# Attention scores in pairs of PSUM banks, the head norm's multiply on GpSimd, and low-order weights over all 128 rows

## Chip, cores and metric

The kernel runs on one core of a Trainium2 chip. The metric is the device time of one execution in microseconds; lower is better.

## What is computed

One inference step of one encoder layer, on 1024 prompt rows and 64 sample rows of width 1024. The normalised input goes through one input projection; its columns feed two groups of heads, whose gated outputs go through one output projection:

```
A) differential attention, 8 heads (q1, q2, k1, k2 of 64, value of 128), chunks of 64 seen block-causally:
   s   = q_c . k_c / 8            c = 0, 1      masked by chunk
   p_c = softmax(s)                             over up to 1024 keys (sample: 64 + 128 cached)
   o   = (p_0 - lam * p_1) @ v
   o   = rms_norm(o) * subln * (1 - lambda_init) * silu(gate)
B) RWKV-7 mixing, 16 heads of 64:
   decay = f(w0 + tanh(wd) @ w_up)      a = sigmoid(a0 + ad @ a_up)      (wd, ad of rank 64)
   a matrix state per head is updated row by row with decay, a, k, v; its output is normed and gated
```

## The kernel before

One stream of instructions per engine is written out ahead of time by a planner, the class `Weave`: generators (streams with a rank) yield a delay or a condition, the planner runs the ready stream of lowest rank, and `spend` and `op_` tell it what a piece costs TensorE or another engine. So the order on each engine's queue is fixed when the kernel is built, and the planned costs decide it. On the chip each queue runs in order.

Phase B comes first. `unit` (n = 0 to 16) handles one pair of B heads and one half of 512 prompt rows, 16 units in all, and one unit for the sample rows. A unit computes decay and rate, inverts its chunk matrices, and then walks a chain of 8 chunks, in which TensorE (`cbank`, L804, L821, L832) and VectorE (`gsb` L818, `suv` L827, L828, L842) answer each other. Units overlap. The `filler` stream has the lowest rank: it puts the input projections of both groups (`proj_cm`, L215 to L217, 384 or 320 columns a matmul) between the steps of the units.

The decay and rate inputs are matrix products in two parts. `xw` holds the high part of tanh(wd) in rows 0 to 63 and its low part in rows 64 to 127; `xa` holds the rate input with the halves the other way about. The weights `t` hold w_up and a_up twice, once in each half of the rows: slices 0 and 1 are the rounded weights, slices 2 and 3 what the rounding left. Line 513 multiplies the rounded weights over all 128 rows, line 514 the remainders over the 64 rows `r` of the input's high part.

Phase A follows. For each of 8 heads, `prep` loads q, k, v and the gate and splits q and k into two parts each (`qs`, `k1`, `k2`, L1244 to L1252; map 0 on VectorE, map 1 on GpSimd). Each head has 9 tiles of queries: `qt` 0 to 7 sees 128 to 1024 keys, and `qt` 8 is the sample with 192. `score` runs once for each tile and map c: keys in pieces of up to 512, each piece in one PSUM bank of a pool of four (`pss`), two matmuls a piece (L1322, L1323), a masking memset (L1330), a maximum per piece (L1332), for two pieces the minimum of the two negated maxima (L1337), and an exponential per piece (L1348) that also sums its row. `at["free"]` counts banks for the planner. `qtile` then joins the two maps: for two pieces it adds their sums (L1364), takes reciprocals, combines the maps (`e`, L1370), transposes the weights in blocks of 128 (L1381) into `wt` (L1385), multiplies with the values (L1395), scales (L1403), squares and sums (L1407), makes the norm on GpSimd (`ms`, L1409, L1410), and multiplies by it on VectorE (L1412). After 4 tiles `on` is transposed (L1419) and gated (L1424).

`out_projection` fills the gaps of phase A and the time after it: weights and mixed rows are loaded and split (`wor`, `mxr`, L157 and L158), and multiplied (L1145 to L1147, 512 columns a matmul).

Of the kernel before, what the change touches and what calls it, by code (L numbers as in the profile page):

```python
# [11 lines left out]
F32 = mybir.dt.float32  # L12
# [46 lines left out]
class Weave:  # L59
# [13 lines left out]
    def spend(self, ns):  # L73
        self.now += ns
# [207 lines left out]
def phase_b(tc, I, O, E):  # L282
# [8 lines left out]
    with ExitStack() as bs:  # L291
# [184 lines left out]
        def unit(n, p, hf):  # L476
# [21 lines left out]
            for q0 in range(0, 8, 4) if smp else (0,):  # L498
                if smp:
                    ups = [load_up(q) for q in range(q0, q0 + 4)]  # L500
                    yield W_DMA
                for i, raw in enumerate(ups):
                    ups[i] = t = t512(dt=F32R, nm=f"wus{u}{q0 + i}").rearrange("p (s c) -> p s c", c=P)
                    nc.scalar.copy(t[:, 0:2], raw[:, 0:2])
                    op_(ACT, 256)
                    gtt(t[:, 2:4], raw[:, 0:2], t[:, 0:2].bitcast(F32), op=SUB)
                    d = op_(POOL, 256)
                yield d
                for q, t in enumerate(ups):
                    for j, (x, r) in enumerate(((xw, slice(0, 64)), (xa, slice(64, 128)))):  # L510
                        o_ = pss2[j][:, (q0 + q) * CH:(q0 + q + 1) * CH] if smp else pss2[j]
                        cl = slice(TP, T) if smp else slice(hf * HALF, (hf + 1) * HALF)
                        mm(o_, t[:, j], x[:, cl], start=True, stop=False)
                        mm(o_, t[r, 2 + j], x[r, cl], start=False, stop=True)
                spend(900)

            sq = t512(nm=f"sq{u}")
# [646 lines left out]
def phase_a(tc, I, O, E):  # L1164
# [7 lines left out]
    QW = 9 * P  # L1172

    ap_ = E["ctx"].enter_context(tc.tile_pool(name="ap", bufs=1, reuse_waits="tile"))
    pss = E["ctx"].enter_context(tc.tile_pool(name="pss", bufs=4, space=PSUM, reuse_waits="tile"))
    psx = E["ctx"].enter_context(tc.tile_pool(name="psx", bufs=2, space=PSUM, reuse_waits="tile"))


# [30 lines left out]

    H = {}  # L1210
    ready = set()
    at = {"s": 0, "free": 4}

    def prep(h):
        yield lambda: h in projected and {("q", h // 4), ("k", h // 4)} <= roped and (h == 0 or (h - 1, 1) in ready) and at["s"] >= 18 * (h - 1) + 10
# [87 lines left out]
    ons = {}  # L1303
    turned, summed = set(), set()

    def score(i, h, qt, c, st):

        k0, n = (0, (qt + 1) * P) if qt < 8 else (TP, TS + PAST)
        u = f"{h}_{qt}{c}"
        j = 2 * i + c  # L1310
        parts = [(o_, min(512, n - o_)) for o_ in range(0, n, 512)]
        m = len(parts)
        yield lambda: at["s"] == j and at["free"] >= m and (h, c) in ready
        at["free"] -= m
        at["s"] = j + 1
        qs, k1, k2 = H[h][0:3]
        ss = []
        lq = qs[c][:, qt * P:(qt + 1) * P]
        for o_, w in parts:
            s = pss.tile([P, 512], F32, tag="s", name=f"s{u}{o_}")  # L1320
            ss.append(s)
            mm(s[:, 0:w], lq, k1[c][:, k0 + o_:k0 + o_ + w], start=True, stop=False)  # L1322
            mm(s[:, 0:w], lq, k2[c][:, k0 + o_:k0 + o_ + w], start=False, stop=True)  # L1323
            spend(w / 1.2 + 20)
        yield LA
        nb = ap_.tile([P, 3], F32, tag=f"nb{c}", bufs=3, name=f"nb{u}")
        for i_, (s, (o_, w)) in enumerate(zip(ss, parts)):
            if qt < 8 and i_ == m - 1:

                nc.vector.memset(s[0:64, w - 64:w], -(2.0 ** 100))  # L1330
                op_(DVE, 60)
            nc.vector.tensor_reduce(nb[:, i_:i_ + 1], s[:, 0:w], axis=AX.X, op=MAX, negate=True)  # L1332
            d = op_(DVE, w)
        mx = nb[:, m - 1:m]
        if m > 1:
            mx = nb[:, 2:3]
            vtt(mx, nb[:, 0:1], nb[:, 1:2], op=ALU.min)  # L1337
            d = op_(DVE, 60)
        yield d
        yield lambda: i < 2 or i - 2 in turned  # L1340
        if "sm" not in st:
            st["sm"] = ap_.tile([P, 2], F32, tag="sm", bufs=3, name=f"sm{u}")
            if m > 1:
                st["sp"] = ap_.tile([P, 2, 2], F32, tag="sp", bufs=3, name=f"sp{u}")
        e = ap_.tile([P, 1024], F32, tag=f"e{c}", bufs=2, name=f"e{u}")
        for i_, (s, (o_, w)) in enumerate(zip(ss, parts)):
            sm = st["sm"][:, c:c + 1] if m == 1 else st["sp"][:, c, i_:i_ + 1]
            act(e[:, o_:o_ + w], s[:, 0:w], AF.Exp, bias=mx, accum_out=sm)  # L1348
            d = op_(ACT, w + 50)
            weave.later(d, free_s)  # L1350
        yield d
        st[c] = e

    def free_s():
        at["free"] += 1
# [1 line left out]
    def qtile(i, h, qt, st):  # L1357
        n = (qt + 1) * P if qt < 8 else TS + PAST
        kbs = [(b * P, P, b) for b in range(qt + 1)] if qt < 8 else [(0, TS, 8), (TS, PAST, 9)]
        u = f"{h}_{qt}"  # L1360
        yield lambda: 0 in st and 1 in st
        w_, e1, sm = st[0], st[1], st["sm"]
        if "sp" in st:
            nc.vector.tensor_reduce(sm, st["sp"], axis=AX.X, op=ADD)  # L1364
            op_(DVE, 60)
        ri = ap_.tile([P, 2], F32, tag="ri", bufs=3, name=f"ri{u}")
        nc.vector.reciprocal(ri, sm)
        co = ap_.tile([P, 1], F32, tag="co", bufs=3, name=f"co{u}")
        vts(co, sm[:, 0:1], nlam, ri[:, 1:2], op0=MUL, op1=MUL)
        stt(w_[:, 0:n], e1[:, 0:n], co, w_[:, 0:n], op0=MUL, op1=ADD)  # L1370
        op_(DVE, 400)
        yield op_(DVE, n)
        yield lambda: (h, 2) in ready
        vn, ga = H[h][3:]
        yield lambda: i < 2 or i - 2 in summed
        wt = ap_.tile([P, 8, P], F32, tag="wt", bufs=2, name=f"wt{u}")
        for b0 in range(0, len(kbs), 4):
            sub = kbs[b0:b0 + 4]
            ps = yield from xps(f"wt{u}{b0}")
            for b, (o_, w, _) in enumerate(sub):  # L1380
                nc.tensor.transpose(ps[0:w, b * P:(b + 1) * P], w_[:, o_:o_ + w], ident)  # L1381
            spend(112 * len(sub))
            yield LA
            if qt < 8:
                (nc.vector.tensor_copy if b0 == 0 else nc.scalar.copy)(  # L1385
                    wt[:, b0:b0 + len(sub), :], ps[:, 0:len(sub) * P].rearrange("p (k q) -> p k q", q=P))
            else:
                for b, (o_, w, _) in enumerate(sub):
                    nc.vector.tensor_copy(wt[0:w, b, :], ps[0:w, b * P:(b + 1) * P])
            d = xdone(op_(DVE if b0 == 0 else ACT, P * len(sub)))  # L1390
        turned.add(i)
        yield d
        ops = yield from xps(f"o{u}")
        for b, (o_, w, vb) in enumerate(kbs):
            mm(ops[:, 0:P], wt[0:w, b, :], vn[0:w, vb, :], start=(b == 0), stop=(b == len(kbs) - 1))  # L1395
        spend(230 * len(kbs))
        summed.add(i)
        yield LA
        j = qt // 4
        if (h, j) not in ons:  # L1400
            ons[h, j] = ap_.tile([P, 4, P], F32, tag="on", bufs=3, name=f"on{u}")
        on = ons[h, j][:, qt % 4, :]
        act(on, ops[:, 0:P], AF.Copy, scale=ri[:, 0:1])  # L1403
        yield xdone(op_(ACT, P))
        sq = ap_.tile([P, P], F32, tag="osq", name=f"osq{u}")
        ms = ap_.tile([P, 1], F32, tag="ms", bufs=3, name=f"ms{u}")
        act(sq, on, AF.Square, accum_out=ms)  # L1407
        yield op_(ACT, P)
        gts(ms, ms, 1.0 / P, SUBLN_EPS, op0=MUL, op1=ADD)  # L1409
        gtt(ms, ms, nh[:, 0:1], op=POW)  # L1410
        yield op_(POOL, 270)
        vts(on, on, ms, None, op0=MUL)  # L1412
        d = op_(DVE, P)
        if qt in ((3, 7, 8) if h < 7 else (0, 4, 8)):
            yield d
            m = 4 if qt < 8 else 1
            ps = yield from xps(f"z{u}")
            for b in range(m):
                nc.tensor.transpose(ps[:, b * P:(b + 1) * P], ons[h, j][:, b, :], ident)  # L1419
            spend(112 * m)  # L1420
            yield LA
            n_ = HALF if qt < 8 else TS
            y = ap_.tile([P, HALF], F32, tag="y", name=f"y{u}")
            stt(y[:, 0:n_], ps[:, 0:n_], hsl, ga[:, j * HALF:j * HALF + n_], op0=MUL, op1=MUL)  # L1424
            xdone(op_(DVE, n_))
            nc.sync.dma_start(out=mixd["A", j][h * P:(h + 1) * P, :], in_=y[:, 0:n_])
            yield 3000
            mixed.add((f"A{h}", j))

    for h in range(8):  # L1430
        weave.add(10 * h + 9.5, prep(h))
        for o_, qt in enumerate((0, 1, 8, 2, 3, 4, 5, 6, 7) if h < 7 else (7, 6, 5, 4, 3, 2, 1, 0, 8)):
            st = {}
            weave.add(10 * h + o_, qtile(9 * h + o_, h, qt, st))
            for c in range(2):
                weave.add(10 * h + o_ + 0.1 * c + 0.1, score(9 * h + o_, h, qt, c, st))
    weave.run(lambda: not weave.live)


# [57 lines left out]
```

## Time and profile before

| what | value |
|---|---|
| median of 3 runs | 1876.28 us (1874.08 to 1876.33) |
| the profiled execution | 1870.95 us, span 1869.1 us |
| mean granted TensorE clock | 0.975 |
| busy: TensorE, weight loads, VectorE, ScalarE, GpSimd | 91%, 80%, 70%, 46%, 37% |
| phase B, attention, the rest of the output projection | about 0 to 1240, 1260 to 1740, 1740 to 1869 us |

A matmul's record begins when its columns enter the array; records of neighbours overlap, since matmuls are pipelined. So the distance from start to start is what a matmul costs the engine, not the length of its record. PE stands for TensorE, PEld for its weight loads, DVE for VectorE, ACT for ScalarE and POOL for GpSimd.

### The profile page before, as it was taken

The numbers are of one execution on the slowest core, as the hardware profiler recorded it, in microseconds if no ns is written. First come the engines' busy times: TensorE is split into PE (matmuls) and PEld (weight loads), VectorE is DVE, ScalarE is ACT, GpSimd is POOL, SyncE is SP. The second block draws the span as 40 slices with busy tenths as digits, with TensorE's granted clock in tenths as the row PEclk, the third lists the DMA queues.
The fourth block names the chain that finished last, engine by engine and source line by source line (L and its number), as shares of the span: only waits on it lengthen the run. The fifth ranks groups of instructions, "written<-read, shape, count | busy, mean of one in ns | idle before, by whom it ended". The sixth has DMA issues, their size and how long they took to land. (4 is left out here: it accounts for less than half of the span.)

```text
span 1869.1 us, 34871 instructions
## 1 busy us (share of the span) xinstructions
PE 1699.6 (91%) x12930; PEld 1500.6 (80%) x12930; DVE 1305.8 (70%) x2892; ACT 868.1 (46%) x2155; POOL 695.4 (37%) x866
## 2 busy tenths in 40 slices
PE   6999899999998999999999899977899798889995
PEld 5888888888888888888888789877778676777784
DVE  5568777777778787886875766524687667787336
ACT  5534444344344444444443433323566576676323
POOL 4442333233233323323332421212332356554657
PEclk9999999999999999999999999998999899899998
DMA  4110111321122111110101121345555565443325
GB/s 144 49 55 27 50 48 48 80 82 36 39 72 62 51 44 35 52 38 29 57 26 50 57 62 50 106 118 160 153 156 149 165 155 156 121 131 105 116 87 181
DMA packets 204244, 158.85 MB, mean 85 GB/s; under 512 B 44229, under 2 KB 185194, under 8 KB 204074
## 3 DMA queue, kind: packets, MB, share of 16 engines
q1 hardware_dynamic: 169242, 137.33, 25.5%
q10 hardware_dynamic: 34832, 19.30, 4.0%
q8 instruction: 102, 1.67, 0.4%
q14 instruction: 68, 0.56, 0.1%
HBM read 108.67 MB, written 47.34 MB: 83 GB/s over the span
## 5 line engine op out<-in xcount | busy, mean ns | idle before, releaser
L1348 ACT ACTIVATE e<-s,nb 128x512 f32<-128x512 f32 (+4 forms) x208 | 117.3, 569 | 59.3 <-DVE nb L1332 26.1
L1145 PE MATMUL po<-woh,mxh 128*128 128x512 f32 x288 | 120.3, 419 | 7.1 <-DVE part L1156 5.9
L1147 PE MATMUL po<-wol,mxh 128*128 128x512 f32 x288 | 115.9, 402 | 3.9 <-DVE nb L1337 2.5
L1146 PE MATMUL po<-woh,mxl 128*128 128x512 f32 x288 | 115.5, 401 | 4.2 <-POOL mxl L158 4.2
L1332 DVE TENSOR_REDUCE nb<-s 128x1 f32<-128x512 f32 (+4 forms) x208 | 108.0, 529 | 15.9 <-PE s L1323 14.6
L158 POOL TENSOR_TENSOR mxl<-mxr,mxh 128x512 fp32r<-128x512 f32 (+1 forms) x72 | 88.3, 1231 | 74.9 <-ACT mxh L157 61.8
L811 ACT ACTIVATE sd<-suv,dc 64x64 f32<-64x64 f32 x128 | 44.4, 347 | 154.1 <-DVE suv L842 149.4
L1322 PE MATMUL s<-k,qs 128*128 128x512 f32 (+4 forms) x208 | 78.9, 385 | 22.0 <-ACT k L1249 10.0
L1395 PE MATMUL x_o<-vn,wt 128*128 128x128 f32 (+1 forms) x608 | 88.0, 289 | 10.1 <-DVE wt L1385 5.4
L1395 PEld LDWEIGHTS x_o<-vn,wt 128*128 128x128 f32 (+1 forms) x608 | 81.0, 200 | 18.5 <-issue 5.5
L1156 DVE TENSOR_TENSOR part<-po,part 128x512 f32<-128x512 f32 x72 | 49.5, 688 | 55.6 <-PE po L1147 55.5
L842 DVE SCALAR_TENSOR_TENSOR suv<-cbank,dc,sd 64x64 f32<-64x64 f32 x224 | 63.0, 281 | 33.3 <-PE cbank L832 29.2
L832 PE MATMUL cbank<-suv,bkt 128*128 128x128 f32 x256 | 56.9, 304 | 32.0 <-DVE suv L828 32.0
L832 PEld LDWEIGHTS cbank<-suv,bkt 128*128 128x128 f32 x256 | 41.1, 190 | 45.7 <-DVE suv L828 43.4
L215 PE MATMUL pj_v<-hhi,wh_v 128*128 128x384 f32 (+1 forms) x192 | 70.1, 365 | 6.5 <-DVE mg L416 6.1
L1409 POOL TENSOR_SCALAR ms<-ms 128x1 f32<-128x1 f32 x72 | 18.0, 249 | 150.9 <-ACT osq L1407 150.4
L1323 PE MATMUL s<-k,qs 128*128 128x512 f32 (+4 forms) x208 | 71.5, 358 | 2.4 <-POOL k L1252 1.5
L215 PE MATMUL pj_av<-hhi,wh_av 128*128 128x384 f32 (+1 forms) x192 | 70.2, 365 | 3.0 <-DVE fl_g L939 3.0
L157 ACT CAST mxh<-mxr 128x512 fp32r<-128x512 f32 (+1 forms) x72 | 40.7, 567 | 68.7 <-PE po L1147 29.4
L677 POOL TENSOR_TENSOR ltlo<-lt,lt 64x512 f16<-64x512 f32 x32 | 37.7, 1177 | 93.4 <-ACT lt L665 92.2
L1145 PEld LDWEIGHTS po<-woh,mxh 128*128 128x128 f32 x288 | 55.4, 192 | 20.6 <-DVE part L1156 4.4
L215 PE MATMUL pj_k<-hhi,wh_k 128*128 128x384 f32 (+1 forms) x192 | 67.7, 352 | 4.0 <-ACT raw_k L230 4.0
(533 smaller groups left out, 6189.5 us busy)
## 6 DMA issues: line engine op xcount, KB each, us to landing
mxr<-mixB SPq DMA_DIRECT2D x32, 256.0 KB
wor<-in_w_out SPq DMA_DIRECT2D x64, 128.0 KB
qa<-scr_q SPq DMA_DIRECT2D x32, 204.0 KB
ka<-scr_k SPq DMA_DIRECT2D x32, 204.0 KB
scr_q<-fl_q SPq DMA_DIRECT2D x8, 544.0 KB
scr_k<-fl_k SPq DMA_DIRECT2D x8, 544.0 KB
scr_v<-fl_v SPq DMA_DIRECT2D x8, 544.0 KB
scr_g<-fl_g SPq DMA_DIRECT2D x8, 544.0 KB
```

Of the source, the lines that this page charges most:

```text
L158: gtt(lo, raw, hi.bitcast(F32), op=SUB)
L215: mm(ps[:, :n], hi[:, k, :], hhi[i][:, k, :], start=(k == 0), stop=False)
L832: mm(s, bkt[:, c], suv[:, c], start=True, stop=True)
L842: stt(suv[r, c + 1, h, :] if c < 7 and not smp else to[r], s[r, h * CH:(h + 1) * CH], dc[r, c:c + 1], sd[r], op0=MUL, op1=ADD)
L1145: mm(ps, hi[:, q, :], wh, start=(q == 0), stop=False)
L1146: mm(ps, lo[:, q, :], wh, start=False, stop=False)
L1147: mm(ps, hi[:, q, :], wl, start=False, stop=(q == len(ks) - 1))
L1322: mm(s[:, 0:w], lq, k1[c][:, k0 + o_:k0 + o_ + w], start=True, stop=False)
L1323: mm(s[:, 0:w], lq, k2[c][:, k0 + o_:k0 + o_ + w], start=False, stop=True)
L1332: nc.vector.tensor_reduce(nb[:, i_:i_ + 1], s[:, 0:w], axis=AX.X, op=MAX, negate=True)
L1348: act(e[:, o_:o_ + w], s[:, 0:w], AF.Exp, bias=mx, accum_out=sm)
L1395: mm(ops[:, 0:P], wt[0:w, b, :], vn[0:w, vb, :], start=(b == 0), stop=(b == len(kbs) - 1))
```

## The change

Three edits. Line 514 uses all 128 rows of the remainder weights and of the input, so the low part of the input is multiplied by them too. In `score`, the pool holds two tiles of two banks instead of four of one: for tiles of up to 512 keys both maps go into one tile, one bank each, with one memset and one maximum over both and then an exponential for each; for 640 to 1024 keys one map fills both banks, with one maximum and one exponential over all keys, so lines 1337 and 1364 go. The multiply by the norm (line 1412) moves from VectorE to GpSimd, to which the planner gives a cost of its own.

```diff
-                    for j, (x, r) in enumerate(((xw, slice(0, 64)), (xa, slice(64, 128)))):
+                    for j, x in enumerate((xw, xa)):
...
-                        mm(o_, t[r, 2 + j], x[r, cl], start=False, stop=True)
+                        mm(o_, t[:, 2 + j], x[:, cl], start=False, stop=True)
...
-    pss = E["ctx"].enter_context(tc.tile_pool(name="pss", bufs=4, space=PSUM, reuse_waits="tile"))
+    pss = E["ctx"].enter_context(tc.tile_pool(name="pss", bufs=2, space=PSUM, reuse_waits="tile"))
...
-    at = {"s": 0, "free": 4}
+    at = {"s": 0, "free": 2}
...
-        yield lambda: at["s"] == j and at["free"] >= m and (h, c) in ready
-        at["free"] -= m
-        at["s"] = j + 1
+        yield lambda: at["s"] == 2 * i + cs[0] and at["free"] and (h, cs[-1]) in ready
+        at["free"] -= 1
+        at["s"] += m
...
+        s2 = pss.tile([P, 1024], F32, tag="s", name=f"s{u}")
+        for c in cs:
+            lq = qs[c][:, qt * P:(qt + 1) * P]
+            for o_ in range(0, n, 512):
+                w = min(512, n - o_)
+                b = (c * 512 if m > 1 else 0) + o_
+                mm(s2[:, b:b + w], lq, k1[c][:, k0 + o_:k0 + o_ + w], start=True, stop=False)
+                mm(s2[:, b:b + w], lq, k2[c][:, k0 + o_:k0 + o_ + w], start=False, stop=True)
+                spend(w / 1.2 + 20)
         yield LA
...
+        s3 = s2.rearrange("p (c k) -> p c k", c=m)
+        nb = ap_.tile([P, 2], F32, tag="nb", bufs=4, name=f"nb{u}")
+        if qt < 8:
+            nc.vector.memset(s3[0:64, :, n - 64:n], -(2.0 ** 100))
+            op_(DVE, 60 * m)
+        nc.vector.tensor_reduce(nb[:, 0:m], s3[:, :, 0:n], axis=AX.X, op=MAX, negate=True)
+        yield op_(DVE, m * n)
...
+        for j, c in enumerate(cs):
+            st[c] = e = ap_.tile([P, 1024], F32, tag=f"e{c}", bufs=2, name=f"e{u}{c}")
+            act(e[:, 0:n], s3[:, j, 0:n], AF.Exp, bias=nb[:, j:j + 1], accum_out=st["sm"][:, c:c + 1])
+            d = op_(ACT, n + 50)
+        weave.later(d, free_s)
         yield d
...
-        if "sp" in st:
-            nc.vector.tensor_reduce(sm, st["sp"], axis=AX.X, op=ADD)
-            op_(DVE, 60)
...
-        vts(on, on, ms, None, op0=MUL)
-        d = op_(DVE, P)
+        gts(on, on, ms, None, op0=MUL)
+        d = op_(POOL, P // 2)
...
-            for c in range(2):
-                weave.add(10 * h + o_ + 0.1 * c + 0.1, score(9 * h + o_, h, qt, c, st))
+            for cs in ((0,), (1,)) if 4 <= qt < 8 else ((0, 1),):
+                weave.add(10 * h + o_ + 0.1 * cs[0] + 0.1, score(9 * h + o_, h, qt, cs, st))
```

## Rows read from the trace of the kernel before

**Rows 1.** Busy time by stretch: us, then PE, PEld, DVE, ACT, POOL, clock, DMA

```profile
500.00:600.00 100.00, 93.26 (x847) 82.86 (x845) 78.33 (x170) 43.64 (x99) 33.25 (x44) 1.00 0.25 71
...
1400.00:1500.00 100.00, 88.57 (x568) 78.44 (x567) 73.53 (x208) 63.19 (x196) 36.22 (x54) 0.95 0.56 155
```

**Rows 2.** Waits of TensorE in phase B: us in total, times, longest

```profile
PE cbank L832 <- DVE suv L828: 32.0, 36, 3.2
```

**Rows 3.** Timeline of TensorE around lines 513 and 514 of one unit: start, us

```profile
66.09 0.40 PE L513 MATMUL m_up<-xw,t_wus 128*128 128x512 f32 x1
66.41 0.50 PE L514 MATMUL m_up<-xw,t_wus 64*128 64x512 f32 x1
66.84 0.50 PE L513 MATMUL m_up<-xa,t_wus 128*128 128x512 f32 x1
67.27 0.50 PE L514 MATMUL m_up<-xa,t_wus 64*128 64x512 f32 x1
67.70 0.44 PE L215 MATMUL pj_r<-hhi,wh_r 128*128 128x384 f32 x1
67.98 0.34 PE L216 MATMUL pj_r<-hlo,wh_r 128*128 128x384 f32 x1
68.15 0.34 PE L217 MATMUL pj_r<-hhi,wl_r 128*128 128x384 f32 x1
```

**Rows 4.** Waits of the weight loads in phase B

```profile
PEld m_up L514 <- issue: 8.3, 32, 0.3
```

**Rows 5.** Timeline of TensorE, two neighbouring matmuls of the output projection

```profile
1495.75 0.40 PE L1145 MATMUL po<-woh,mxh 128*128 128x512 f32 x1
...
1495.99 0.39 PE L1146 MATMUL po<-woh,mxl 128*128 128x512 f32 x1
```

**Rows 6.** Timeline of TensorE in the sample unit, first and 17th of a run

```profile
1013.83 0.28 PE L513 MATMUL m_upNone<-xw,t_wusNone 128*128 128x64 f32 x1
...
1017.42 0.44 PE L215 MATMUL pj_av<-hhi,wh_av 128*128 128x384 f32 x1
```

**Rows 7.** Chain that ended last: a run of small matmuls over all rows

```profile
1401.31 1.78 PE x_o L1395 x16
```

**Rows 8.** Groups by line and shape in attention: busy us, mean ns, idle before

```profile
L1348 ACT ACTIVATE e<-s,nb 128x512 f32<-128x512 f32 x96 | 65.8, 688 | 26.7 <-DVE nb L1337 20.1 <-DVE sm L1364 3.0 <-PE s L1323 1.9
L1332 DVE TENSOR_REDUCE nb<-s 128x1 f32<-128x512 f32 x96 | 65.2, 680 | 15.2 <-PE s L1323 14.6
...
L1348 ACT ACTIVATION_READ_ACCUMULATOR e<-s,nb 128x1 f32 x208 | 41.6, 200 | 0.0
...
L1412 DVE TENSOR_SCALAR on<-on,ms 128x128 f32<-128x128 f32 x71 | 29.2, 411 | 39.4 <-POOL ms L1410 34.9 <-ACT k L1249 2.0 <-ACT on L1403 1.8
...
L1337 DVE TENSOR_TENSOR nb<-nb 128x1 f32<-128x1 f32 x64 | 17.9, 279 | 0.5
...
L1348 ACT ACTIVATE e<-s,nb 128x128 f32<-128x128 f32 x32 | 11.6, 364 | 20.9 <-DVE nb L1332 20.9
...
L1332 DVE TENSOR_REDUCE nb<-s 128x1 f32<-128x128 f32 x32 | 8.9, 277 | 0.3
```

**Rows 9.** Groups of GpSimd by line and shape

```profile
L537 POOL TENSOR_SCALAR t_th<-t_th 128x512 f32<-128x512 f32 x16 | 10.4, 652 | 19.6 <-ACT t_th L532 14.1 <-PE m_up L514 5.2
```

**Rows 10.** Waits in attention, all engines: us in total, times, longest

```profile
DVE on L1412 <- POOL ms L1410: 34.9, 31, 5.0
...
PEld s L1322 <- ACT e L1348: 15.5, 27, 5.4
...
PE s L1322 <- ACT e L1348: 9.6, 11, 5.2
```

**Rows 11.** Chain that ended last, at the start of a head's splits

```profile
1618.82 2.68 POOL qs L1246
1622.64 2.80 DVE on L1412
```

**Rows 12.** Busy time by stretch, one of 10 us

```profile
1470.00:1480.00 10.00, 3.40 (x10) 2.33 (x10) 3.33 (x15) 4.41 (x12) 4.50 (x6) 0.61 0.81 276
```

More of the change, by code (lines that the diff above doesn't have):

```diff
@@ L1304, in phase_a, with score @@
     turned, summed = set(), set()
-    def score(i, h, qt, c, st):
+    def score(i, h, qt, cs, st):
         k0, n = (0, (qt + 1) * P) if qt < 8 else (TP, TS + PAST)
[L1309 to L1312, printed above, removed]
-        yield lambda: at["s"] == j and at["free"] >= m and (h, c) in ready
-        at["free"] -= m
-        at["s"] = j + 1
-        qs, k1, k2 = H[h][0:3]
[L1317 to L1324, printed above, removed]
-        yield LA
[L1326 to L1330, printed above, removed]
-                op_(DVE, 60)
[L1332 to L1339, printed above, removed]
@@ new lines, in score @@
+        m = len(cs)
+        u = f"{h}_{qt}{cs[0]}"
+        yield lambda: at["s"] == 2 * i + cs[0] and at["free"] and (h, cs[-1]) in ready
+        at["free"] -= 1
+        at["s"] += m
+        qs, k1, k2 = H[h][0:3]
+        s2 = pss.tile([P, 1024], F32, tag="s", name=f"s{u}")
[7 more added lines that the diff above has]
+                spend(w / 1.2 + 20)
@@ L1342, in score @@
             st["sm"] = ap_.tile([P, 2], F32, tag="sm", bufs=3, name=f"sm{u}")
[L1343 to L1350, printed above, removed]
+        for j, c in enumerate(cs):
[3 more added lines that the diff above has]
+        weave.later(d, free_s)
         yield d
-        st[c] = e
+        st["e"] = st.get("e", 0) + m
     def free_s():
@@ L1360, in qtile @@
         u = f"{h}_{qt}"
-        yield lambda: 0 in st and 1 in st
+        yield lambda: st.get("e") == 2
         w_, e1, sm = st[0], st[1], st["sm"]
-        if "sp" in st:
-            nc.vector.tensor_reduce(sm, st["sp"], axis=AX.X, op=ADD)
-            op_(DVE, 60)
         ri = ap_.tile([P, 2], F32, tag="ri", bufs=3, name=f"ri{u}")
```

## The prediction

> **What bounds the kernel now.** I read the busy time by stretch first. In phase B TensorE is busy 93 of 100 us at the full clock and VectorE 78; in attention it is 89 and 74 [rows 1]. So TensorE bounds both phases, and there are two ways to gain: give it less to do, or shorten its gaps. Next come its waits. In phase B the largest is 32.0 us in 36 pieces, a chain step that waits for VectorE [rows 2]. In attention a hundred us holds 100 - 88.6 = 11.4 us of gaps [rows 1], so about 53 us over the 470 us from 1270 to 1740. Third, since a busy engine needn't be a fast one, I read the timeline around the lines that the diff touches, start to start; there the first edit shows its worth.
>
> **Line 514 over all rows.** The edit adds no matmul and no column. But the four matmuls of a unit start 0.32, 0.43, 0.43 and 0.43 us apart, and the next projection matmul another 0.28 later [rows 3], where matmuls of 512 columns over 128 rows follow each other after 0.24 [rows 5] and the next one of 384 after 0.17 [rows 3]. The listing of weight loads says why: before each of the 32 loads of line 514 in the 16 prompt units the loader stood idle, 8.3 us in all, with nothing to wait for [rows 4]. So the half-height weights were not loaded under the matmul in flight, and the loads after them weren't either. With one height throughout, the stretch from 66.09 to 68.15 shrinks from 2.06 to 4 x 0.24 + 2 x 0.17 = 1.30 us: 0.76 saved, times 16 units, 12.2 us.
>
> In the sample unit, 16 small matmuls take 1017.42 - 1013.83 = 3.59 us [rows 6], 0.224 each; 16 of another line, all over 128 rows, take 1.78 [rows 7]. That saves 1.8 us. The sample's other 16 I count at nothing: their weights come one by one out of GpSimd's split, and TensorE would only wait longer.
>
> The sum is 14.0 us of TensorE time. Not all of it need arrive: where the next step of a chain waits for VectorE, an earlier TensorE waits longer. But TensorE's order in phase B doesn't move (no planned cost there changes), what VectorE works on mostly hangs on TensorE's own steps and so moves with them, and VectorE has 22 of 100 us free. The bounds are nothing (every saved piece ends in a wait) and 14.0; I take 12, near the upper one, since the waits are 32.0 us in 1240 and the saved pieces lie among fillers.
>
> One rule speaks against this edit. The Trainium skill, TensorE: Matmul & The Clock Gate, in Part 3 on packing small matmuls, says that a weight load overlaps a matmul in flight only when its row group differs. By it line 514, whose rows differ from its neighbours', would be the load that is hidden, and the edit would cost instead of save. The trace disagrees: the neighbours of one height run at 0.17 and 0.24 us, the others have the idle time [rows 3 to 5]. The rule has a rival below.
>
> **Maxima and exponentials in pairs.** A head had 26 maxima (5 tiles of one piece, 4 of two, two maps) and gets 13; 104 of 208 go. A maximum over 512 takes 680 ns and over 128 takes 277 [rows 8]: 1.05 ns an element and 143 ns fixed. The elements stay, so 104 x 0.143 = 14.9 us go. The 64 minima go, 17.9 us. The exponentials fall by 64. At 688 and 364 ns [rows 8] they cost 0.844 ns an element and 256 ns fixed, and each reads its accumulator for 200 ns: 64 x 0.456 = 29.2 us of ScalarE. No row shows an instruction across two banks. Its bounds are this line (1024 elements: a maximum of 1.22 us, an exponential of 1.12) and two single ones (1.36 and 1.38); I take the line, as all four points are of the same instructions.
>
> For a long tile the time from the last matmul to the end of the exponentials was 0.68 + 0.28 + 2 x (0.69 + 0.20) = 2.74 us, the first maximum lying under the last matmuls, and becomes 1.22 + 1.12 + 0.20 = 2.54. So the path is about the same; the engines are freer.
>
> **The multiply on GpSimd.** VectorE loses 29.2 us of line 1412 [rows 8] and also the 34.9 us in which its queue stood behind that instruction, waiting for GpSimd's norm, up to 5.0 us at once [rows 10]; the next maxima, the `e` of line 1370 and the `wt` copies were queued behind it. GpSimd made the norm itself, so there the multiply waits for nobody. Its cost has no row: from nothing up to the 652 ns for 512 elements [rows 9]; I take 0.3 us, nearer a quarter than the whole: 72 x 0.3 = 22 us, on an engine that is busy 36 of 100 [rows 1]. Behind it lie the splits of the next weights and head, 0.3 us later each, and the transposes of `on`, at 3 of 9 tiles.
>
> In the chain one such multiply lasted 2.80 us just after GpSimd's split of `qs` [rows 11], against a mean of 0.41. The Trainium skill, SBUF — State Buffer, Who interferes with whom, says that VectorE and GpSimd lock each other out of a shared port pair. That fits this row, and it also says that a GpSimd multiply blocks VectorE's two-input instructions while it lasts. By it, 22 us of the relief could be taken back; the sum would then be some 2 us less.
>
> **What attention gains.** VectorE's occupied time there, some 345 us busy (73.5 of 100) and 35 blocked, falls by 14.9 + 17.9 + 29.2 + 34.9 = 97 us, a quarter. TensorE's gaps are partly others': in one stretch of 10 us no engine is busy over 4.5 us while the DMA engines are 81% busy, and the granted clock averages 0.61, so part ran at 1.2 GHz [rows 12]; that lottery is drawn again, since the order in attention is planned anew. I take a fifth of the 53 us: 11. The bounds are nothing and 53, and on the loss side the rival of the banks.
>
> At each head's start the first tile now waits for both maps' splits. Its cover is the previous head's products and the output projection; uncovered it costs the first map's maximum and exponential, 0.28 + 0.36 + 0.20 = 0.84 us, seven times 6.
>
> **Sum.** 1870.95 (the profiled execution: span 1869.1 and 1.9 around it) - 12 - 11 = 1848. That execution is 5.3 us under the median of 1876.28, so for a median I say **1853 us**.
>
> **Rivals.**
> - *Attention gives nothing.* The gaps belong to loads and copies, or the coarser grants eat the relief. For it: the stretch of [rows 12]; against it: the 34.9 us behind one instruction. 1876.3 - 12 = 1864.
> - *Phase B absorbs its gain* in longer waits of `cbank`. For it: 32.0 us of such waits [rows 2]; against it: they are 2.6% of the phase. 1876.3 - 11 = 1865.
> - *The banks are granted too late*, the other side. Two tiles of scores are in flight as before, but a tile's first bank can't be retaken until all of it is read: 0.56 us later for short pairs (another exponential and its sum), 0.69 for long tiles (2.54 against 0.68 + 0.28 + 0.89 = 1.85). Over 104 grants that is some 65 us if nothing covers it. Today 11 grants of 208 leave TensorE waiting, 9.6 us in all, and 27 delay a weight load [rows 10]. It decides from 23 / 65 = 35% of grants uncovered; at 45% the time is 1876.3 - 23 + 29 = 1882.
> - *The height isn't what costs*, and full-height loads are the exposed ones: 32 more loads with the idle 0.26 us of [rows 4] are 8 us, so 1876.3 + 8 - 11 = 1873. This is how it would go by the Trainium skill's rule above; the trace speaks against it.
>
> **Chances.** Forecast 0.60 (1840 to 1865); attention nothing 0.19; phase B absorbs 0.10; banks 0.07; height 0.04. A difference of 0.2%, 3.8 us, is about what a measurement of this kernel can tell from none. The second and third can slip into it (0.04), the fourth half (0.02): faster 0.87, same 0.06, slower 0.07. The range of 8 in 10 reaches down to both upper terms with a fourth of attention's gaps more (14 + 25: 1837, rounded to 1835) and up past the rivals that keep one gain, with some loss in attention: 1868.
>
> **What would show it.** Right: line 514's matmuls start 0.24 us apart and the idle before their loads is gone; phase B ends about 12 us earlier; VectorE is 60 us less busy and ScalarE 29 less; TensorE's gaps in attention are nearer 40 us than 53. Wrong: the waits on `suv` grow by ten us; TensorE waits for the exponentials (line 1348 of before) at more than a third of the tiles; GpSimd's multiply lasts 0.6 us or the splits of the weights end later than TensorE wants them.

## The result and the profile after

The changed kernel takes 1855.4 us (median; 1852.8 to 1857.0) against 1875.2 for the kernel before on the same chip: ratio 0.9899, interval 0.9876 to 0.9921. The forecast was 1853, the gain 23 us; measured are 20. The profiled execution has a span of 1853.3 us, 15.8 less than before. The last step of phase B's units (the matmuls of `m_zt`) starts for the last time 4.5 us earlier, at 1228.5 us, and the remaining 11 us come after it, from attention and the output projection that fills its gaps.

The busy time by stretch of the changed kernel, columns as in [rows 1]:

```profile
500.00:600.00 100.00, 92.98 (x827) 83.27 (x826) 77.47 (x170) 44.59 (x102) 32.61 (x44) 0.98 0.26 72
...
1400.00:1500.00 100.00, 88.72 (x534) 76.97 (x533) 66.13 (x137) 61.03 (x170) 43.76 (x64) 0.88 0.56 155
```

VectorE is 7 us lighter in the second stretch and GpSimd 8 us heavier. Over the span VectorE falls from 1305.8 to 1254.4 us busy and ScalarE from 868.1 to 849.8; GpSimd rises from 695.4 to 737.2. The whole of attention from 1270 to 1740 us, first of the kernel before, then of the changed one:

```profile
1270.00:1740.00 470.00, 417.97 (x2527) 357.25 (x2527) 343.49 (x894) 292.90 (x879) 204.94 (x263) 0.96 0.52 141
```

```profile
1270.00:1740.00 470.00, 430.96 (x2574) 370.05 (x2574) 292.73 (x589) 279.76 (x756) 260.17 (x350) 0.95 0.53 145
```

TensorE's gaps there fell from 52.0 to 39.0 us, near the 40 that the prediction named as a sign of being right.

The timeline of TensorE around the decay and rate inputs of the first unit (one line lower in the file, so L514 and L515):

```profile
66.75 0.40 PE L514 MATMUL m_up<-xw,t_wus 128*128 128x512 f32 x1
66.99 0.39 PE L515 MATMUL m_up<-xw,t_wus 128*128 128x512 f32 x1
67.22 0.39 PE L514 MATMUL m_up<-xa,t_wus 128*128 128x512 f32 x1
67.44 0.39 PE L515 MATMUL m_up<-xa,t_wus 128*128 128x512 f32 x1
67.67 0.34 PE L215 MATMUL pj_r<-hhi,wh_r 128*128 128x384 f32 x1
67.84 0.34 PE L216 MATMUL pj_r<-hlo,wh_r 128*128 128x384 f32 x1
68.02 0.34 PE L217 MATMUL pj_r<-hhi,wl_r 128*128 128x384 f32 x1
```

Against [rows 3], the same seven starts now lie within 1.27 us instead of 2.06, and the idle time of [rows 4] has no row any more. In the sample unit, the first of the 16 small matmuls and the one behind them:

```profile
1009.53 0.28 PE L514 MATMUL m_upNone<-xw,t_wusNone 128*128 128x64 f32 x1
...
1011.32 0.42 PE L215 MATMUL pj_av<-hhi,wh_av 128*128 128x384 f32 x1
```

They take 1.79 us, against 3.59 in [rows 6]. So TensorE was given back 16 x 0.79 + 1.80 = 14.4 us. Its waits in the chains of phase B:

```profile
PE cbank L833 <- DVE suv L829: 36.1, 36, 3.2
...
PE cbank L822 <- DVE gsb L819: 10.9, 13, 1.8
...
PE cbank L805 <- DVE suv L843: 2.9, 4, 1.2
```

The first was 32.0 us before [rows 2], and the other two:

```profile
PE cbank L821 <- DVE gsb L818: 7.7, 9, 1.8
...
PE cbank L804 <- DVE suv L842: 2.2, 2, 1.2
```

Together they are 8.0 us more, so over half of what was given back is waited away.

Groups of instructions in attention, as in [rows 8]:

```profile
L1401 POOL TENSOR_SCALAR on<-on,ms 128x128 f32<-128x128 f32 x72 | 47.4, 658 | 7.3
...
L1340 ACT ACTIVATION_READ_ACCUMULATOR e<-s,nb 128x1 f32 x144 | 28.9, 201 | 0.0
...
L1333 DVE TENSOR_REDUCE nb<-s 128x1 f32<-128x1024 f32 x16 | 19.5, 1222 | 0.3
...
L1340 ACT ACTIVATE e<-s,nb 128x1024 f32<-128x1024 f32 x16 | 18.0, 1126 | 0.0
```

Instructions over two banks follow the line through the shorter ones (1.22 and 1.12 us were forecast). The multiply on GpSimd takes 0.66 us, not 0.3. The waits of attention:

```profile
DVE s L1331 <- PE s L1324: 54.8, 39, 9.3
...
PEld s L1323 <- ACT e L1340: 13.4, 15, 2.7
...
PE s L1323 <- ACT e L1340: 8.6, 7, 2.2
```

VectorE's longest wait used to be the multiply behind GpSimd's norm [rows 10]. Now it is the scores themselves: VectorE waits for TensorE. And the banks are waited for no more than before (9.6 and 15.5 us).

### The profile page after: what moved, and what is told of

It reads as the page before. It is cut to its first block, busy times and chain, and to the rows that moved or that the text cites. A ratio compares the mean times of both kernels' runs of the same rounds, so it can differ in the third digit from the quotient of the medians.

```text
span 1853.3 us, 34474 instructions
## 1 busy us (share of the span) xinstructions
PE 1691.8 (91%) x12930; PEld 1505.7 (81%) x12930; DVE 1254.4 (68%) x2588; ACT 849.8 (46%) x2027; POOL 737.2 (40%) x938
## 5 line engine op out<-in xcount | busy, mean ns | idle before, releaser
L1340 ACT ACTIVATE e<-s,nb 128x128 f32<-128x128 f32 (+7 forms) x144 | 101.0, 706 | 35.2 <-DVE nb L1333 19.7
L1333 DVE TENSOR_REDUCE nb<-s 128x1 f32<-128x640 f32 (+8 forms) x104 | 95.8, 922 | 2.2
L1384 PEld LDWEIGHTS x_o<-vn,wt 128*128 128x128 f32 (+1 forms) x608 | 80.1, 199 | 19.9 <-DVE wt L1374 5.8
L157 ACT CAST mxh<-mxr 128x512 fp32r<-128x512 f32 (+1 forms) x72 | 40.9, 569 | 74.5 <-PE po L1148 32.2
L215 PE MATMUL pj_aq<-hhi,wh_aq 128*128 128x384 f32 (+1 forms) x192 | 70.0, 365 | 0.5 <-DVE fl_g L940 0.3
```

The lines of the kernel that those rows point to most:

```text
L215: mm(ps[:, :n], hi[:, k, :], hhi[i][:, k, :], start=(k == 0), stop=False)
L1333: nc.vector.tensor_reduce(nb[:, 0:m], s3[:, :, 0:n], axis=AX.X, op=MAX, negate=True)
L1340: act(e[:, 0:n], s3[:, j, 0:n], AF.Exp, bias=nb[:, j:j + 1], accum_out=st["sm"][:, c:c + 1])
```

## The experiments

Each ratio is against runs of the kernel before on the same chip, with its 95% interval. 0.1% is 1.9 us. The theory after the result: the rows edit is worth less than its 14 us, since phase B's chains take part of it back; attention gains since VectorE and ScalarE are lighter. The rivals: the rows edit is worth its 12, and attention's gain is little or the luck of a new order.

### The parts alone

**Line 514 over all rows, alone.** The diff is the first two hunks of the change.

> The kernel before with line 514 over all rows alone. Theory (phase B pays back part of the saved TensorE time in waits for VectorE): 3 to 7 us faster, waits of cbank on VectorE some 6 to 8 us longer than the 42 us before. Rival (the saving arrives and the profiled execution of the changed kernel only had a long stretch at 1.2 GHz): 10 to 14 us faster. Either way the four matmuls start 0.22 to 0.24 us apart.

Measured: 0.9973 (0.9958 to 0.9988), 5 us. The waits in phase B of this run:

```profile
PE cbank L832 <- DVE suv L828: 35.5, 36, 3.2
PE cbank L821 <- DVE gsb L818: 10.7, 13, 1.6
```

They grew by 6.5 us, and with the third one (L804, 2.6 us) by 6.9. That leaves 14.4 - 6.9 = 7.5 us, inside the interval of 2 to 8 us, so the waits can account for what didn't arrive: the edit is worth about a third of the time that it gives back, and the waits of the changed kernel belong to it. The rival is out by the clock too: the granted clock averaged 0.973 over the 12 runs of this kernel, as over the 23 of the kernel before on the same chip. About half of the growth lies at one place, around the sample unit (1000 to 1040 us); first before, then in this run:

```profile
PE cbank L832 <- DVE suv L828: 0.9, 1, 0.9
```

```profile
PE cbank L832 <- DVE suv L828: 4.1, 2, 3.2
```

**Scores in pairs of banks, alone.** The changed kernel with line 514 undone and

```diff
-        gts(on, on, ms, None, op0=MUL)
-        d = op_(POOL, P // 2)
+        vts(on, on, ms, None, op0=MUL)
+        d = op_(DVE, P)
```

> The kernel before with the two-bank scores alone (multiply on VectorE, line 514 over half the rows). If fewer and longer instructions are what attention gains from: 6 to 9 us faster. If the multiply's place is what counts, and the grants cost what the rest saves: within 4 us of before. Phase B unchanged to 1 us.

Measured: 1.0069 (1.0042 to 1.0096), 13 us slower; neither was expected. In attention, TensorE's longest wait and VectorE's:

```profile
PE x_o L1384 <- DVE wt L1374: 14.7, 10, 3.1
```

```profile
DVE on L1401 <- POOL ms L1399: 76.2, 45, 10.2
```

VectorE stood 76 us behind the multiply (37.8 before, in the same stretch), and TensorE waited 14.7 us for copies of `wt` where it had waited 5.4. That the copies came late because they were queued behind the multiply is argued, not shown. The banks weren't it: TensorE waited 1.2 us for exponentials.

**The multiply on GpSimd, alone.** The last hunk of `qtile` on the kernel before.

> The kernel before with the norm's multiply on GpSimd alone. If VectorE's queue standing behind that multiply was what stopped TensorE: 5 to 9 us faster. If GpSimd's 0.66 us each (47 us in all) delays the splits as much: within 3 us of before. Phase B unchanged.

Measured: 1.0019 (1.0002 to 1.0036), no gain. TensorE's waits in attention:

```profile
PE s L1322 <- ACT e L1348: 13.4, 12, 5.2
...
PE x_wt L1381 <- ACT kt L1298: 6.3, 2, 3.7
PE s L1323 <- POOL k L1252: 5.6, 2, 4.1
PE po L1147 <- POOL wol L158: 5.6, 2, 3.6
```

VectorE holds TensorE for 17 us less, but ScalarE and GpSimd for 19 us more (the table below has the sums). The clock may have a part in it: it averaged 0.969 over the 12 runs of this kernel and 0.973 over the 23 of the kernel before.

**Both edits of attention.** The changed kernel with line 514 undone.

> The changed kernel with line 514 over half the rows again: both edits of attention alone. Theory: 11 to 15 us faster than before, so that the rows edit is left with about 5. Rival (the saving of phase B arrives in full): 5 to 9 us faster.

Measured: 0.9946 (0.9925 to 0.9967), 10 us faster. Two edits that lose 13 and 4 us alone gain 10 together. To see why, I added up all rows of TensorE's waits from 1270 to 1760 us by the engine that ended them:

| kernel | VectorE | ScalarE | GpSimd | sum, us | ratio |
|---|---|---|---|---|---|
| before | 28.8 | 17.7 | 6.5 | 53.0 | 1 |
| scores alone | 36.0 | 13.2 | 6.6 | 55.8 | 1.0069 |
| multiply alone | 11.5 | 27.1 | 16.4 | 55.0 | 1.0019 |
| both edits of attention | 11.6 | 22.1 | 9.3 | 43.0 | 0.9946 |
| all three edits | 10.3 | 19.9 | 7.9 | 38.1 | 0.9899 |

The table can be read like this: the multiply's move takes 17 us from VectorE's column and the next engine in the path takes them over, unless the pairs have shortened ScalarE's and VectorE's work as well. That is a reading and not shown. The sums are from one execution each, and the run with the order drawn again (below) has 12.5, 15.8 and 17.1, in all 45.4 us, at the same time as the 38.1, so a difference of 7 us says little.

Between the last two rows lies line 514 alone: put onto both edits of attention it gives 9 us (3 to 15), where it gave 5 on the kernel before.

### What attention's gain hangs on

**The multiply on VectorE, placed later.** On the kernel of scores alone:

```diff
-        yield op_(POOL, 270)
+        yield op_(POOL, 270) + 3000
```

> Scores in pairs of banks with the multiply on VectorE, as in the run of scores alone, but the planner places the multiply 3 us later on VectorE's queue. Theory (that run lost because VectorE's queue stood 76 us behind the multiply, which waits for GpSimd's norm): the wait falls under 25 us and the time comes back by 13 to 25 us, to 0.99 to 1.00 of before. Rival (the two-bank grants or a bad order cost it): it stays at 1.005 to 1.01 of before, whatever the wait does.

Measured: 1.0000 (0.9987 to 1.0013). The 13 us came back, with the same pairs of banks, so it wasn't the pairs that cost them. But the wait did not go as expected:

```profile
DVE on L1401 <- POOL ms L1399: 62.3, 40, 7.4
```

It fell only to 62 us, and what TensorE waits for VectorE to 26.9 us (36.0 with the multiply early). So the sum of VectorE's waits isn't the price; it matters where they lie. The order changed with the delay, so this run doesn't separate the two.

**The order drawn again.** The changed kernel with

```diff
-LA, LAT, W_LD, W_DMA = 130, 100, 11000, 3122
+LA, LAT, W_LD, W_DMA = 140, 100, 11000, 3122
```

> The changed kernel with nothing else than the planner's delay LA at 140 instead of 130 ns, so that the order in attention is drawn again. If the gain of attention is the lighter engines': within 4 us of the changed kernel (0.988 to 0.992 of before). If it is the luck of an order: anywhere from 0.985 to 1.005.

Measured: 0.9906 (0.9886 to 0.9926). One other order gives the same time, so the whole change doesn't rest on a single lucky one. For the run of scores alone this wasn't tried.

### What phase B takes back

**A dose of TensorE work.** On the changed kernel, after line 515:

```diff
+                        if not smp:
+                            mm(o_, t[:, j], x[:, cl], start=True, stop=False)
+                            mm(o_, t[:, 2 + j], x[:, cl], start=False, stop=True)
```

> The changed kernel with the four matmuls of the decay and rate inputs issued twice in each of the 16 prompt units (the second four overwrite the first with the same values): 16 x 4 x 0.23 = 14.7 us more TensorE work at the same places. If phase B passes on about a third of what is saved there: 4 to 7 us slower than the changed kernel. If TensorE bounds it outright: 13 to 15 us slower.

Measured: 0.9965 (0.9951 to 0.9979), that is 0.0066 above the changed kernel, 12 us (7 to 17). So 14.7 us more cost 12, and 14.4 us less gave 5 (2 to 8). The waits of this run:

```profile
PE cbank L836 <- DVE suv L832: 34.8, 35, 4.0
...
PE cbank L825 <- DVE gsb L822: 7.6, 9, 1.7
```

Together they are 42.4 us, between the 39.7 of the kernel before and the 47.0 of the changed one. Phase B seems to pass on more of what is added than of what is saved: with less TensorE work the chains' answers come too late, with more they are covered. The intervals only just part, and by the 9 us that line 514 gives on both edits of attention they don't.

**The sample unit's loads on SyncE's queue.** On the changed kernel:

```diff
-        def load_up(q):
+        def load_up(q, eng=nc.scalar):
...
-                    nc.scalar.dma_start(out=t[r:r + 64, s, :], in_=I[nm][0, :, q * P:(q + 1) * P])
+                    eng.dma_start(out=t[r:r + 64, s, :], in_=I[nm][0, :, q * P:(q + 1) * P])
...
-                    ups = [load_up(q) for q in range(q0, q0 + 4)]
+                    ups = [load_up(q, nc.sync) for q in range(q0, q0 + 4)]
```

> The changed kernel with the sample unit's 16 weight loads issued on SyncE's queue instead of ScalarE's, where issuing them holds ScalarE back 9.1 us and TensorE 3.2 us at 1019 us. If that stall and the half clock behind it took back a part of phase B's saving: 3 to 8 us faster than the changed kernel, the wait of cbank at that place gone. If not: within 2 us of it.

Measured: 0.9880 (0.9856 to 0.9903), 3.6 us below the changed kernel by the ratios; the intervals overlap. The busy time by stretch around the sample unit, first of the kernel before, then of the changed one, then of this one:

```profile
1010.00:1040.00 30.00, 29.06 (x234) 25.95 (x234) 14.42 (x33) 9.25 (x22) 10.51 (x13) 0.89 0.15 48
```

```profile
1010.00:1040.00 30.00, 25.96 (x193) 23.68 (x193) 13.87 (x30) 8.18 (x21) 8.09 (x11) 0.72 0.17 54
```

```profile
1010.00:1040.00 30.00, 28.79 (x270) 26.01 (x269) 19.68 (x41) 10.83 (x25) 9.97 (x13) 0.83 0.17 54
```

TensorE is busy 28.8 us of these 30 instead of 26.0, at a granted clock of 0.83 instead of 0.72 (the three don't do the same work in this stretch). The longest wait of `cbank` from 1000 to 1040 us fell from 3.2 to 1.4 us.

**The same loads on the kernel before.** The same diff.

> The kernel before with the sample unit's weight loads on SyncE's queue, nothing else. If that stall took back a part of the rows edit, it was covered before, and this run is within 2 us of before. If the loads cost ScalarE and TensorE time in any case: 3 to 6 us faster than before, and the gain of the same edit on the changed kernel says nothing about the rows edit.

Measured: 0.9984 (0.9970 to 0.9998), 3 us faster. So the loads cost some time in any case (1 to 6 us), and by the ratios, 3.0 and 3.6 us, the run before it says nothing of the rows edit.

The traces say more. On the kernel before, issuing these loads held ScalarE for 9.0 us too, but `cbank` waited only 0.9 us at that place; with line 514 over all rows it waited 4.1. So the stall was covered and the rows edit uncovered it. And the move lets the last `m_zt` start 7.3 us earlier on the changed kernel (1221.2 against 1228.5 us), but 2.2 us earlier on the kernel before (1230.8 against 1233.0); in the four kernels that differ from the one before in attention alone, it starts from 1231.1 to 1233.5. That leans to the loads taking back some 5 us of the rows edit. The times of whole runs don't show it and these are single executions, so it stays open.

**VectorE lighter in phase B.** The kernel before without the token shift of r, k and v, then the same with line 514 over all rows:

```diff
-                else:
+                elif idx == 24:
                     stt(d, raw[:, t0:t0 + n], mu, d, op0=MUL, op1=ADD)
```

> The kernel before without the prompt's token shift of r, k and v (48 instructions of VectorE at 0.75 us, 36 us in phase B, are left out, so those three inputs are not mixed with the row before them). It is the base for the next run. If VectorE paces phase B's chains: 5 to 15 us faster than before; if TensorE does: within 4 us.

Measured: 1.0005 (0.9990 to 1.0020). VectorE is 39 us less busy up to 1240 us (859 for 898), the two waits of `cbank` shown above fall from 39.7 to 32.2 us, and the time is the same. But the clock isn't: it averaged 0.9695 over the 12 runs of this kernel and 0.973 over the 29 of the kernel before, and in the profiled executions it was 0.98 against 1.00 from 400 to 1000 us. Among runs of the kernel before, 0.001 of clock went with 0.7 to 1.3 us on the three chips, so by an estimate 2 to 5 us may be hidden there. Why the clock fell isn't shown. So this run doesn't settle whether VectorE's load paces phase B.

> The same with line 514 over all rows. Theory (the rows edit's 14 us of TensorE time were partly paid back because VectorE was late): with VectorE 36 us lighter the edit is worth 8 to 13 us against the run without shift. Rival (what took it back is not VectorE's load, but fixed delays of the chains, the half clock and the sample unit's loads): 3 to 6 us, as alone.

Measured: 0.9960 (0.9943 to 0.9978), so 0.9955 of the run without shift, 8 us. Waits of the first and of the second:

```profile
PE cbank L832 <- DVE suv L828: 28.2, 29, 3.2
PE cbank L821 <- DVE gsb L818: 4.0, 8, 0.8
```

```profile
PE cbank L832 <- DVE suv L828: 31.1, 29, 3.1
PE cbank L821 <- DVE gsb L818: 5.2, 12, 0.8
```

Here the clock is alike, 0.9695 and 0.969 on average. With VectorE lighter the rows edit lengthens the waits by 4.1 us instead of 6.5 and is worth 8 us (4 to 13) instead of 5. That leans to the theory that VectorE's late answers take the saving back, but each ratio is uncertain by 3 us, and so the two don't part for certain.

### The fastest

**The changed kernel with the loads on SyncE's queue and LA at 140 ns.**

> The changed kernel with the sample unit's loads on SyncE's queue and the planner's delay at 140 ns: the fastest two versions together. If the attention order and the loads are independent: 0.985 to 0.989 of before. If both runs were the same kernel plus chance: 0.989 to 0.992.

Measured: 0.9858 (0.9835 to 0.9880), 1847.8 us: the fastest of all runs, some 8 us under the changed kernel by the ratios.

## Why the prediction was right, and where its size was off

**TensorE bounds both phases.** Shown for phase B: 14.7 us more for it there cost 12. No run adds or takes TensorE work in attention, so there it isn't shown.

**Line 514.** The cause and its price were right: 0.79 us a unit (0.76 forecast) and 1.80 in the sample unit (1.8). The mis-sized term is what arrives of the sum: I took 12 of 14.0 us, from waits of 32.0 us in 1240. Alone the edit gives 5, and phase B's last step came 4.5 us earlier instead of 12, since three waits of the chain grew by 6.9 us (8.0 in the changed kernel). The argument that what VectorE works on moves along with TensorE was wrong in that place; a wait that is small now says how much is uncovered today, not how much lies just under the cover. The rival in which phase B absorbs its gain was the better half of the truth. What makes VectorE's answers late is known for one place, where ScalarE is held by the sample unit's loads (3.2 of the 6.9 us). For the rest it stays open: with 39 us less load the waits fell, but the time did not, at a lower clock.

**The rule on weight loads.** Here loads of one height run under the matmul in flight and those of another height didn't: after the edit the four start 0.22 to 0.24 us apart, before 0.32 to 0.43. So the rival in which full-height loads are the exposed ones is out. The Trainium skill, TensorE: Matmul & The Clock Gate, Part 3, lets a load overlap a matmul in flight only where row groups differ, and the trace disagrees. In its paragraph on the mechanism the same part of the Trainium skill also lets a load go ahead where it targets the background weight buffer, which the prediction passed over. No run here shows which buffer a load used.

**Maxima and exponentials.** Prices as forecast: 1222 ns against 1.22 us and 1126 ns against 1.12 us. Added up by instruction, the exponentials lose 16.3 us and their accumulator reads 12.7, the 29 us of the forecast. Yet ScalarE's busy time fell by 18 us and VectorE's by 51, not by 29 and 60: records of neighbours overlap on these engines too (an exponential of 0.69 us is followed by its accumulator read after 0.59), so the sum of records counts more than the engine was occupied.

**The multiply.** 0.66 us against the 0.3 taken, just past the upper bound of 0.652. In the changed kernel that cost little: TensorE's waits for GpSimd are 7.9 us, 6.5 before. Alone they were 16.4, and the move gained nothing. The 22 us that VectorE's two-input instructions might lose beside it do not show: the largest of them, line 1370 (line 1359 after), took 67.9 us in all before and 59.6 after.

**Attention's gain.** 11 us were taken and both edits together gave 10 (6 to 14). But the prediction added up the reliefs of two edits, and neither gains alone: the scores lost 13 us with the multiply placed early and nothing with it placed later, the multiply lost up to 7. As far as the sums of waits show, what the multiply's move frees goes to ScalarE's and GpSimd's waits unless the scores are lighter too. The size was right and the step that led to it, a share of the occupied time, was too simple; that it came out at 10 is in part luck.

**The banks.** The rival on the other side is out: TensorE waits 8.6 us for exponentials in the changed kernel and 9.6 in the one before. The two parts alone multiply to 0.9973 x 0.9946 = 0.9919, inside the interval of the whole. The total came out 3 us from the forecast because phase B's miss of 7 was offset in part by what the whole gives beyond its parts, which the intervals don't show to be real. So the closeness of the total is luck.

## What to carry to other kernels

Read start to start, not record lengths: a matmul over half the rows between ones over all of them cost 0.2 us at each change of height (0.11 where they had 64 columns), and no busy share shows it. Taking an instruction from the engine that holds others up need not help when the next engine in the path has no room, as the multiply alone suggests; so test edits together as well as alone, in both signs. Look at the granted clock before calling two equal times a proof: the kernel without the token shift ran at a lower one. And count a saving on the bound engine in full only where no chain answers to it: here 12 of 14.7 us of added work arrived, and 5 to 9 of 14 us saved, in three pairs of runs.

## What the runs showed of the hardware

GpSimd's multiply of 128x128 by a column took 611 ns at the median, where its operation with fixed numbers on 128x512 took 621 at the median (652 on average, [rows 9]): a quarter of the elements hardly cost less, in another form of the operands. VectorE did the same multiply in 285 ns at the median and 2.8 us at the longest. Where the sample unit left TensorE waiting 3.2 us in the changed kernel, the granted clock was 0.50 from 1030 to 1040 us, the level of 1.2 GHz. But with the loads on SyncE's queue, where the longest wait was 1.4 us, it was 0.56 from 1020 to 1030 us, so the runs don't show that the longer wait brought the clock down. And issuing its 16 loads back to back kept ScalarE from its next step for 9.1 us.
